# Two layers of a hybrid decoder trunk: rotary halves swapped by transfers, retention state by masked whole-array products, another order of products and steps

## The chip, the core and the metric

The kernel runs on one core of one Trainium2 chip. A core has a tensor engine (PE), a vector engine (DVE), a scalar engine (ACT), a general engine (POOL, GpSimd), and a synchronisation engine (SP) that here only issues transfers (DMAs). Each engine works through its own queue in order; semaphores hold an instruction back until what it needs from another engine or from a transfer is there. Matrix products read SBUF and write one of eight banks of PSUM; DVE and ACT read the banks. The metric is the device time of one execution in microseconds; smaller is better.

## What is computed

Two layers, each with three sub-layers on a sequence of 512 positions and a width of 1024, in float32. The mixing sub-layer has three kinds of heads:

```python
z = rmsnorm(x, mix_pre_g[i]) @ w_in[i]
# A: gated spatial mixing in chunks of 128
# B: retention, chunkwise, 6 heads of 64, with rotary positions
rq = rotary(r_q, positions); rk = rotary(r_k, positions) * 64 ** -0.5
...
def rotary(t, positions):
    ...
    t1, t2 = t[..., :half], t[..., half:]
    return jnp.concatenate([t1 * cos - t2 * sin, t1 * sin + t2 * cos], axis=-1)
def step(R, inp):      # one chunk of the retention
    q_i, k_i, v_i = inp
    inner = jnp.einsum('bhtd,bhsd->bhts', q_i, k_i) * decay
    o = jnp.einsum('bhts,bhse->bhte', inner, v_i)
    o = o + jnp.einsum('bhtd,bhde->bhte', q_i, R) * q_decay
    R = R * chunk_decay + jnp.einsum('bhsd,bhse->bhde', k_i * k_decay, v_i)
    return R, o
# C: forgetting attention, 6 heads of 64, blocks of 128 queries
x = x + rmsnorm(concat(A, B, C) @ w_o[i], mix_post_g[i])
f = conv_gated_mlp(rmsnorm(x, ffn_pre_g[i]), w_gate, w_up, conv_w, conv_b, w_down)
x = x + rmsnorm(f, ffn_post_g[i])
gate = sigmoid(rmsnorm(x, ple_pre_g[i]) @ w_ple_gate[i])
x = x + rmsnorm((p[i] @ w_ple_proj[i]) * gate, ple_post_g[i])
```

The output is x after the two layers, 512 x 1024.

## The kernel before

**A planner writes the order.** The code of `body` (L541) calls engine functions through `Plan.engine` (L138), which only records each operation with its dependencies and an estimated cost. `Plan.issue` (L252) then plays a list schedule: among the operations that are ready, an engine takes the one recorded first, and an operation that needs a new tile may be taken only if the tile's first use lies at most `AHEAD[stage]` operations (L62) behind the oldest operation not yet done, and if a buffer is free. The order that comes out is issued on L452, which is why every line of the profile says L452; operations are told apart by the names of their tiles. What is recorded earlier thus has precedence, and the engines' queues are fixed when the program is built. `fence` (L86) makes PE keep the recorded order; this holds for blocks 4 to 30 of the feed-forward part.

**Products.** Every large product splits its float32 operands in a high and a low part (`split`, L657: one ACT copy, one DVE subtraction) and takes three matmuls for one (`mm3`, L932). Pairs of projections that share their input go through `seven` (L869): seven block products in place of eight, on sums of weight blocks (`seven_weights`, L846: two 512 KB loads on SP, two adding loads on POOL's queue, sums and splits on DVE and ACT) and on sums of inputs (`Seven`, L763; `Mixed.combine`, L735). Three banks are used: beta takes b11, then h6 on top, then h7, then h4; alpha takes b21; gamma takes hd, then b22. Between the products ACT or DVE copies a bank's partial result out, and the next product on the same bank waits for that copy. In the feed-forward part some down products (`pieces`, L1322) run between b22 and h4.

**The mixing stage** (`mixers`, L965) takes its steps in the order of `STEPS` (L494): u (gating projection), F (fox values), H (sums of inputs), f0 to f2 (fox projections of head pairs), g and G (retention gates), r0 to r2 (retention projections of head pairs with the rotary turn), v (retention values), a0 to a2 (fox attention), L (silu), s (spatial gating), c0 to c2 (retention core).

- `ret_proj` (L1133): after `seven`, q and k lie as 128 partitions (two heads of 64) x 512 positions, tiles `rm`. For the rotary turn ACT writes the exchanged halves into a tile `rr`, four operations of 32 partitions for each of q and k, two of them with a minus sign (L1139, L1140); three DVE operations follow, `m*cos`, `r*sin`, and their sum.
- `ret_core` (L1146): for three chunks and two heads, a 64 x 64 state product on a part of the array (`kvps`, L1177), then a memset, a copy and two scaled sums for each head build R, whose off-diagonal blocks are zero (L1179 to L1184). R is then read by a 128x128 product for both heads.

**Output projection** (`out_proj`, L1244): chunks in the order `O_CHUNKS` (0, 2, 1, 3); the residual rows x are loaded by chunk 0, 1, 2, 3, two chunks to a buffer. After the first chunk the weights of feed-forward block 0 are asked for (`EARLY`, L496). **Feed-forward part** (`ffn`, L1274): 32 blocks of 128 columns, each one call of `seven` with some eighth part of a down product.

Of the kernel before, what the change touches and what calls it, by code (L numbers as in the profile page):

```python
# [50 lines left out]
class Plan:  # L51
# [7 lines left out]

    SETS = {"X": 17, "W": 7}  # L60

    AHEAD = {"mix": 416, "wo": 450, "wo2": 381, "emb": 503, "gu0": 443, "gu": 478, "dn": 673, "end": 164, "pg": 300, "pg2": 392}  # L62
    LOAD = 1290
    TICK = 10240 / 3
    PHASE = 1900
# [405 lines left out]
def constants():  # L471
    idx = np.arange(P, dtype=np.float64)
    lg = np.log(1.0 - 2.0 ** (-5.0 - np.arange(6, dtype=np.float64)))
    diff = idx[None, :] - idx[:, None]
    decay = np.where(diff >= 0, np.exp(lg[:, None, None] * np.maximum(diff, 0.0)), 0.0) / 8.0
    qdec = np.exp(lg[:, None] * (idx + 1.0))
    kdec = np.exp(lg[:, None] * (P - 1.0 - idx)) / 8.0
    cd = np.exp(lg * P)
    hf = np.repeat(np.arange(2), 64)
    c = {}  # L480
    c["ident"] = np.eye(P)
    c["decay"] = decay.transpose(1, 0, 2).reshape(P, 6 * P)
    c["qdec"] = np.stack([qdec[2 * p + hf] for p in range(3)], 1).reshape(P, 3 * P)
    c["kdec"] = kdec.T
    c["cd"] = np.stack([cd[2 * p + hf] for p in range(3)], 1)
    c["invf"] = (10000.0 ** (-np.arange(32, dtype=np.float64) / 32))[np.arange(P) % 32][:, None]
    c["cum"] = np.concatenate([(idx[:, None] <= idx[None, :]).astype(np.float64), np.ones((P, P))], 1)
    c["mask"] = np.where(idx[None, :] <= idx[:, None], 0.0, 1e30)
    return {k: np.ascontiguousarray(v.astype(np.float32)) for k, v in c.items()}

PAIRS = [(c + p * P, d + p * P) for c, d in ((C_RQ, C_RK), (C_FK, C_FQ)) for p in range(3)] + [(C_RG, C_RG + P)]
STEPS = "u F H f0 g f1 r0 a0 v a1 G L s r1 r2 c0 f2 c1 c2 a2"  # L494
O_CHUNKS = (0, 2, 1, 3)
EARLY = {0: 0}  # L496
O_ORDER = (5, 6, 0, 1, 2, 3, 4, 7)
IDLE = 16
SUMS_BY_DMA = True
# [41 lines left out]
def body(ctx, tc, a, out):  # L541
# [42 lines left out]


    class Rows:
        def __init__(self, src):
            self.src, self.t = src, [None, None]

        def load(self, c, queue=SY):  # L590
            if self.t[c // 2] is None:
                self.t[c // 2] = b8("x", (2, D))
            queue.dma_start(out=self[c], in_=self.src[:, c, :])

        def __getitem__(self, c):
            return self.t[c // 2][:, c % 2, :]

    x0 = a["x"][0].rearrange("(c p) d -> p c d", p=P)
    xd = [dram(f"x{i}", (P, NCH, D)) for i in range(3 * DEPTH - 1)]
# [208 lines left out]
    def post_part(src, g, out):  # L808

        n = src.shape[-1]  # L810
        s1 = small("s1", 1, bufs=12)
        A.activation(junk_t[:, 0:n], src, AF.Square, scale=D ** -0.5, accum_out=s1)
        V.tensor_tensor(out=out, in0=src, in1=g, op=ALU.mult)
        return s1
# [51 lines left out]
        split(sb[:, 0, :], sb[:, 1, :], raw[:, 1024:2048])  # L866
        return wg, wu, sa, sb

    def seven(h, ws, gs, us, scale=1.0, between=None):  # L869

        wg, wu, sa, sb = ws
        be, al, ga = (bank(n)[:, 0:256] for n in ("beta", "alpha", "gamma"))
        t1, t2 = slice(0, 256), slice(256, 512)

        def product(ps, w, n, first, last, part=range(4)):
            for k in part:
                ks = slice(k * P, k * P + P)
                mm3(ps, lambda i: w[i][:, ks], lambda i: h.part(n, i, k), first and k == 0, last and k == 3, True)

        def part(t, i):  # L880
            return [t[:, j, i * 512:i * 512 + 512] for j in range(2)]
        product(be, part(wg, 0), "b11", True, False)
        vbe, val, vga = (in_order(t) for t in (be, al, ga))
        g1, g2, u1, u2 = (halves(t[:, ts]) for t in (gs, us) for ts in (t1, t2))
        A.copy(g1, vbe)
        product(al, part(wg, 1), "b21", True, True)
        V.tensor_tensor(out=g1, in0=val, in1=g1, op=ALU.add)
        product(be, part(sa, 0), "h6", False, False)
        A.copy(g2, vbe)
        product(ga, part(sa, 1), "hd", True, False)  # L890
        if scale == 1.0:
            A.copy(u2, vga)
        else:
            A.mul(u2, vga, -scale)
        product(be, part(sb, 0), "h7", False, False)
        V.scalar_tensor_tensor(out=u2, in0=vbe, scalar=-scale, in1=u2, op0=ALU.mult, op1=ALU.subtract if scale == 1.0 else ALU.add)
        product(ga, part(sb, 1), "b22", False, True)
        V.tensor_tensor(out=g2, in0=vga, in1=g2, op=ALU.add)
# [66 lines left out]
    def mixers(l, hT, uv, ready):  # L965
# [8 lines left out]
        av = m4[:, 1024:2048].rearrange("p (c n) -> p c n", c=NCH)  # L974
        cst = m5[0:6, 0:512]
        mask = m5[:, 512:640]
        cosT = m5[:, 1536:2048]
        decay, qdec, cum, sinT = m6[:, 0:768], m6[:, 768:1152], m6[:, 1152:1408], m6[:, 1408:1920]
        for t, n in ((decay, "decay"), (qdec, "qdec"), (cum, "cum"), (mask, "mask")):
# [153 lines left out]
        def ret_proj(p):  # L1133
            res = [wk("rm") for _ in range(2)]
            seven(hT, seven_weights(a["w_fm"][l, p]), *res)
            for m in res:
                r = wk("rr")
                for s in (0, 64):
                    A.mul(r[s:s + 32, :], m[s + 32:s + 64, :], -1.0)  # L1139
                    A.copy(r[s + 32:s + 64, :], m[s:s + 32, :])  # L1140
                V.tensor_tensor(out=m, in0=m, in1=cosT, op=ALU.mult)
                V.tensor_tensor(out=r, in0=r, in1=sinT, op=ALU.mult)
                V.tensor_tensor(out=m, in0=m, in1=r, op=ALU.add)
            return res

        def ret_core(p, q, k):  # L1146
# [25 lines left out]
            kvp = bank("kvps")  # L1172
            with plan.together():
                for c in range(NCH - 1):
                    for s in range(2):
                        h = 2 * p + s
                        T.matmul(kvp[s * 64:s * 64 + 64, c * 64:c * 64 + 64], lhsT=kt[:, c * P + s * 64:c * P + s * 64 + 64], rhs=rv[:, c, h * 64:h * 64 + 64], start=True, stop=True)  # L1177
            R = wk("R", (P, 3, P))
            for s in range(2):  # L1179
                fs, off = slice(s * 64, s * 64 + 64), slice(64 - s * 64, P - s * 64)  # L1180
                G.memset(R[fs, :, off], 0.0)
                V.tensor_copy(R[fs, 0, fs], kvp[fs, 0:64])
                for c in (1, 2):
                    V.scalar_tensor_tensor(out=R[fs, c, fs], in0=R[fs, c - 1, fs], scalar=cd[fs, p:p + 1], in1=kvp[fs, c * 64:c * 64 + 64], op0=ALU.mult, op1=ALU.add)  # L1184
            ps = bank("rops")
            with plan.together():
                for c in range(NCH):
# [56 lines left out]
    def out_proj(l, cc, ready, x, new, g, nxt):  # L1244

        plan.stage = "wo"
        f = [b8("fo", (2, D)) for _ in range(2)]
        u = tm_units(a["w_wo"][l, 0], 512)
        first = [bank("wo0") for _ in range(NCH)]
        for j, k in enumerate(O_ORDER):  # L1250
            for c in range(NCH):
                tm_mm(first[c], cc, k, c, u, j == 0, j == KB - 1, j=j)
        plan.stage = "wo2"
        u = tm_units(a["w_wo"][l, 1], 512)
        plan.stage = "emb"
        emb = embed_operands(l, range(2) if l else (1,))
        plan.stage = "wo2"
        for c in range(NCH):
            x.load(c)
        first = [post_part(ps, g[:, 0, 0:512], f[c // 2][:, c % 2, 0:512]) for c, ps in enumerate(first)]  # L1260

        def done(c, ps):
            fr = f[c // 2][:, c % 2, :]
            post_chunk(x[c], (first[c], post_part(ps, g[:, 0, 512:1024], fr[:, 512:1024])), fr, stored=new[:, c, :])
            nxt(c, x[c])
            if len(seen) in EARLY:
                ready[EARLY[len(seen)]] = gate_up_weights(l, EARLY[len(seen)])
            seen.append(c)

        seen = []  # L1270
        tm_chunk_major(cc, u, 512, done, O_ORDER, O_CHUNKS)
        return emb

    def ffn(l, hs, emb, ready, x, new, g, nxt):  # L1274
# [10 lines left out]
        def gate_up(b, between):  # L1285
            ws = gate_up_weights(l, b) if b not in ready else ready[b]
            gs, us = wk("gs"), wk("us")
            seven(hs, ws, gs, us, between=between)

            cv = wk("cv")  # L1290
            A.activation(cv, gs, AF.Identity, bias=cw[:, 3, b:b + 1], scale=cw[:, 2, b:b + 1])
# [224 lines left out]
    for l in range(DEPTH):  # L1516
# [4 lines left out]
        emb = out_proj(l, cc, ready, Rows(src), xd[3 * l], g, hs)  # L1521
# [36 lines left out]
```

## Time and profile before

| | us |
|---|---|
| median of 3 runs (1526.79 to 1529.71) | 1526.82 |
| the profiled execution | 1528.62 |
| its span, first to last instruction | 1526.9 |
| start, embedding of layer 0 and first norms | 0 to 59 |
| mixing stage, layer 0 | 59 to 190 |
| output projection, layer 0 | 190 to 244 |
| feed-forward part, layer 0 | 244 to 722 |
| third sub-layer, layer 0 | 722 to 805 |
| mixing and output projection, layer 1 | 805 to 1000 |
| feed-forward part and third sub-layer, layer 1 | 1000 to 1527 |

A page of the profile gives busy times over the whole span; the stages have different limits, so the view of busy time by stage is read first, and in a stage the waits. In lines of the timeline the columns are start, duration, engine, operation, output<-inputs, shapes, count, and in brackets the idle time of the engine before it and what ended it. In the chain of waits a line is start, length and what the time was spent on. In groups of instructions the part after the first bar is busy time and mean ns, after the second the idle time before and what ended it. float32 products of small tiles appear as two records each.

### The profile page before, as it was taken

The page shows a single profiled execution, that of the slowest core. Times are in us where ns is not written, and L with a number is a line of the kernel's source. Part 1 is how long each engine was busy: PE and PEld are TensorE (multiplying, and loading weights), DVE is VectorE, ACT ScalarE, POOL GpSimd, SP SyncE. Part 2 cuts the span into 40 slices and gives each one's busy share as a digit, 9 for nine tenths or more (in the row PEclk, how much of TensorE's full clock was granted, in tenths as well). Part 3 has the DMA queues.
Part 4 walks back from the last instruction along what each step waited for, and adds up shares of the span by engine and source line. Part 5 has one row for each costly group of instructions (what it writes and reads, how often), then busy time and mean ns, then how long its engine had stood idle before and what let it go on. Part 6 is the DMA issues. An engine that isn't in the chain of part 4 may idle for free.

```text
span 1526.9 us, 26942 instructions
## 1 busy us (share of the span) xinstructions
PE 1496.3 (98%) x10554; PEld 1383.6 (91%) x10554; DVE 1216.7 (80%) x2036; ACT 888.9 (58%) x1501; POOL 194.3 (13%) x233
## 2 busy tenths in 40 slices
PE   8999999999999999999999999999999999999997
PEld 6998888899999999998889887799999999999987
DVE  6888969978778777768797779799688778778685
ACT  8557647755555545545575565587655555455462
POOL 1111102111101111100120102121101011011010
PEclk9999999999999999999999999999999999999999
DMA  9445619735646646556573355295545565465541
GB/s 335 88 135 122 209 52 280 189 90 146 173 90 175 150 117 173 146 155 245 190 197 99 92 146 182 68 334 130 146 117 153 163 149 130 123 174 139 212 174 70
DMA packets 87879, 239.02 MB, mean 157 GB/s; under 512 B 10036, under 2 KB 18364, under 8 KB 87752
## 3 DMA queue, kind: packets, MB, share of 16 engines
q1 hardware_dynamic: 64856, 195.81, 37.6%
q0 software_dynamic: 22464, 40.90, 17.0%
q8 instruction: 83, 1.36, 0.4%
q10 hardware_dynamic: 432, 0.59, 0.1%
q14 instruction: 44, 0.36, 0.1%
HBM read 219.94 MB, written 17.33 MB: 155 GB/s over the span
## 4 chain that ended last, share of the span: by engine, by line
PE 74%; DVE 8%; DMA 5%; ACT 5%; issue 5%; POOL 1%; SPq 0%; POOLq 0%; DVEq 0%; ACTq 0%
PE beta L452 20%; PE dn L452 19%; PE ps L452 13%; PE gamma L452 11%; PE alpha L452 5%; DMA graw<-in_w_gu_dram 3%; DMA traw<-in_w_dn_dram 2%; PE wo L452 1%; ACT rr L452 1%; PE hps L452 1%; DVE cv L452 1%; PE tps L452 1%; PE ops L452 1%; ACT junk L452 1%; POOL y L452 1%
## 5 line engine op out<-in xcount | busy, mean ns | idle before, releaser
L452 PE MATMUL dn<-thl,act 128*128 128x512 f32 x1536 | 351.7, 380 | 0.0
L452 PEld LDWEIGHTS dn<-thl,act 128*128 128x128 f32 x1536 | 281.8, 189 | 35.0
L452 POOL DMA_DIRECT2D graw<-in_w_gu_dram x128 | 112.1, 908 | 733.4 <-DVE wg L452 232.0
L452 PE MATMUL ps<-thl,hT 128*128 128x512 f32 (+3 forms) x984 | 198.7, 358 | 2.5 <-ACT hT L452 2.4
L452 PEld LDWEIGHTS ps<-thl,hT 128*128 128x128 f32 x984 | 171.6, 189 | 19.5 <-ACT hT L452 2.9
L452 DVE TENSOR_TENSOR thl<-traw,thl 128x1024 fp32r<-128x1024 f32 (+3 forms) x124 | 141.8, 1152 | 13.4 <-ACT thl L452 13.3
L452 ACT CAST thl<-traw 128x1024 fp32r<-128x1024 f32 (+3 forms) x124 | 121.2, 995 | 21.2 <-PE dn L452 9.2
L452 PEld LDWEIGHTS beta<-hh,wu 128*128 128x128 f32 x936 | 123.2, 191 | 7.2 <-DVE us L452 1.4
L452 PE MATMUL beta<-hh,wu 128*128 128x256 f32 x936 | 126.2, 275 | 1.0 <-DVE us L452 0.9
L452 PE MATMUL beta<-hh,wsa 128*128 128x256 f32 x936 | 120.6, 277 | 6.1 <-ACT gs L452 3.2
L452 PE MATMUL gamma<-hhd,wsa 128*128 128x256 f32 x936 | 120.8, 277 | 0.9 <-ACT wsa L452 0.8
L452 PEld LDWEIGHTS beta<-hh,wsa 128*128 128x128 f32 x936 | 111.4, 192 | 9.2 <-ACT gs L452 4.4
L452 PE MATMUL beta<-hh,wsb 128*128 128x256 f32 x936 | 118.0, 276 | 0.1
L452 DVE TENSOR_TENSOR graw<-graw 128x512 f32<-128x512 f32 x156 | 106.7, 684 | 10.4 <-DMA graw<-in_w_gu_dram 7.9
L452 PEld LDWEIGHTS gamma<-hhd,wsa 128*128 128x128 f32 x936 | 113.1, 194 | 1.3 <-ACT wsa L452 1.0
L452 PEld LDWEIGHTS beta<-hh,wsb 128*128 128x128 f32 x936 | 111.2, 193 | 0.3 <-ACT gs L452 0.3
L452 ACT CAST wsa<-graw 128x1024 fp32r<-128x1024 f32 x78 | 82.0, 1051 | 43.2 <-PE gamma L452 24.7
L452 DVE TENSOR_TENSOR wg<-graw,wg 128x1024 fp32r<-128x1024 f32 x78 | 95.1, 1219 | 13.0 <-ACT wg L452 12.8
L452 DVE TENSOR_TENSOR wsa<-graw,wsa 128x1024 fp32r<-128x1024 f32 x78 | 95.1, 1219 | 10.0 <-ACT wsa L452 9.9
L452 DVE SCALAR_TENSOR_TENSOR cv<-gs,cw,cv 128x511 f32<-128x511 f32 (+1 forms) x128 | 95.0, 743 | 8.5 <-ACT cv L452 8.2
L452 DVE TENSOR_TENSOR wsb<-graw,wsb 128x1024 fp32r<-128x1024 f32 x78 | 95.0, 1218 | 6.6 <-ACT wsb L452 5.9
L452 ACT CAST wg<-graw 128x1024 fp32r<-128x1024 f32 x78 | 82.1, 1053 | 30.5 <-PE gamma L452 13.2
(225 smaller groups left out, 2620.6 us busy)
## 6 DMA issues: line engine op xcount, KB each, us to landing
graw<-in_w_gu_dram SPq DMA_DIRECT2D x128, 512.0 KB
graw<-in_w_gu_dram POOLq DMA_DIRECT2D x128, 256.0 KB, 5.4
traw<-in_w_dn_dram SPq DMA_DIRECT2D x64, 512.0 KB
x<-x SPq DMA_DIRECT2D x40, 512.0 KB
graw<-in_w_fm_dram SPq DMA_DIRECT2D x28, 512.0 KB
traw<-in_w_wo_dram SPq DMA_DIRECT2D x16, 512.0 KB
traw<-in_w_pg_dram SPq DMA_DIRECT2D x16, 512.0 KB
graw<-in_w_fm_dram POOLq DMA_DIRECT2D x28, 256.0 KB, 5.1
```

Of the source, the lines that this page charges most:

```text
L452: made = o[1](*[self.map(v) for v in o[2]], **{k: self.map(v) for k, v in o[3].items()})
```

## The change

It has five parts.

- **Rotary halves.** The eight ACT operations of a pair's q and k become eight transfers on SP, each 32 partitions x 2 KB from SBUF to SBUF. The minus sign goes into the table of inverse frequencies, so that the sine table has it.
- **Retention state.** Three 128x128 products for both heads replace six 64x64 ones; one DVE product with a 0/1 mask `heads` (a new constant, 64 KB, loaded in each layer) takes the off-diagonal blocks away, and two scaled sums over 128 x 128 follow.
- **Seven products.** From block 4 of the feed-forward part on, hd, h6, b22, h7 replaces h6, hd, h7, b22.
- **Output projection.** x and the result tiles are paired in the order of `O_CHUNKS`, and after the fourth chunk the weights of block 1 are asked for.
- **Step order and limits.** `STEPS` and all ten `AHEAD` values.

```diff
-    AHEAD = {"mix": 416, "wo": 450, "wo2": 381, "emb": 503, "gu0": 443, "gu": 478, "dn": 673, "end": 164, "pg": 300, "pg2": 392}
+    AHEAD = {"mix": 401, "wo": 461, "wo2": 344, "emb": 430, "gu0": 423, "gu": 479, "dn": 552, "end": 208, "pg": 264, "pg2": 401}
...
-    c["invf"] = (10000.0 ** (-np.arange(32, dtype=np.float64) / 32))[np.arange(P) % 32][:, None]
+    c["invf"] = (10000.0 ** (-np.arange(32, dtype=np.float64) / 32))[np.arange(P) % 32][:, None] * np.where(np.arange(P) % 64 < 32, -1, 1)[:, None]
+    c["heads"] = hf[:, None] == hf[None, :]
...
-STEPS = "u F H f0 g f1 r0 a0 v a1 G L s r1 r2 c0 f2 c1 c2 a2"
+STEPS = "u F H f1 f0 r0 a0 v g a1 G L s r1 c0 c1 f2 r2 c2 a2"
-EARLY = {0: 0}
+EARLY = {0: 0, 3: 1}
...
     class Rows:
-        def __init__(self, src):
-            self.src, self.t = src, [None, None]
+        def __init__(self, src, order=range(NCH)):
+            self.src, self.t, self.at = src, [None, None], {c: i for i, c in enumerate(order)}
...
-        product(be, part(sa, 0), "h6", False, False)
-        A.copy(g2, vbe)
-        product(ga, part(sa, 1), "hd", True, False)
...
+        for step in (hd, h6, b22, h7) if apart else (h6, hd, h7, b22):
+            step()
...
-                for s in (0, 64):
-                    A.mul(r[s:s + 32, :], m[s + 32:s + 64, :], -1.0)
-                    A.copy(r[s + 32:s + 64, :], m[s:s + 32, :])
+                for s in range(0, P, 32):
+                    SY.dma_start(out=r[s:s + 32, :], in_=m[s ^ 32:(s ^ 32) + 32, :])
...
-                    for s in range(2):
-                        h = 2 * p + s
-                        T.matmul(kvp[s * 64:s * 64 + 64, c * 64:c * 64 + 64], lhsT=kt[:, c * P + s * 64:c * P + s * 64 + 64], rhs=rv[:, c, h * 64:h * 64 + 64], start=True, stop=True)
+                    cs = slice(c * P, c * P + P)
+                    T.matmul(kvp[:, cs], lhsT=kt[:, cs], rhs=rv[:, c, p * P:(p + 1) * P], start=True, stop=True)
             R = wk("R", (P, 3, P))
-            for s in range(2):
-                fs, off = slice(s * 64, s * 64 + 64), slice(64 - s * 64, P - s * 64)
-                G.memset(R[fs, :, off], 0.0)
-                V.tensor_copy(R[fs, 0, fs], kvp[fs, 0:64])
-                for c in (1, 2):
-                    V.scalar_tensor_tensor(out=R[fs, c, fs], in0=R[fs, c - 1, fs], scalar=cd[fs, p:p + 1], in1=kvp[fs, c * 64:c * 64 + 64], op0=ALU.mult, op1=ALU.add)
+            V.tensor_tensor(out=R, in0=kvp[:, 0:384].rearrange("p (c d) -> p c d", c=3), in1=heads.unsqueeze(1).to_broadcast([P, 3, P]), op=ALU.mult)
+            for c in (1, 2):
+                V.scalar_tensor_tensor(out=R[:, c, :], in0=R[:, c - 1, :], scalar=cd[:, p:p + 1], in1=R[:, c, :], op0=ALU.mult, op1=ALU.add)
...
+        fo = {c: f[i // 2][:, i % 2, :] for i, c in enumerate(O_CHUNKS)}
...
-        for c in range(NCH):
+        for c in O_CHUNKS:
             x.load(c)
...
-            seven(hs, ws, gs, us, between=between)
+            seven(hs, ws, gs, us, between=between, apart=b > 3)
```

More of the change, by code (lines that the diff above doesn't have):

```diff
@@ L586, in body @@
     class Rows:
-        def __init__(self, src):
-            self.src, self.t = src, [None, None]
+        def __init__(self, src, order=range(NCH)):
+            self.src, self.t, self.at = src, [None, None], {c: i for i, c in enumerate(order)}
         def load(self, c, queue=SY):
-            if self.t[c // 2] is None:
-                self.t[c // 2] = b8("x", (2, D))
+            if self.t[self.at[c] // 2] is None:
+                self.t[self.at[c] // 2] = b8("x", (2, D))
             queue.dma_start(out=self[c], in_=self.src[:, c, :])
         def __getitem__(self, c):
-            return self.t[c // 2][:, c % 2, :]
+            return self.t[self.at[c] // 2][:, self.at[c] % 2, :]
     x0 = a["x"][0].rearrange("(c p) d -> p c d", p=P)
@@ L867, in seven_weights, with seven @@
         return wg, wu, sa, sb
-    def seven(h, ws, gs, us, scale=1.0, between=None):
+    def seven(h, ws, gs, us, scale=1.0, between=None, apart=False):
         wg, wu, sa, sb = ws
@@ L887, in seven, with h6, hd, h7 @@
         V.tensor_tensor(out=g1, in0=val, in1=g1, op=ALU.add)
-        product(be, part(sa, 0), "h6", False, False)
-        A.copy(g2, vbe)
-        product(ga, part(sa, 1), "hd", True, False)
[L891 to L898, printed above, removed]
+        def h6():
+            product(be, part(sa, 0), "h6", False, False)
+            A.copy(g2, vbe)
+        def hd():
+            product(ga, part(sa, 1), "hd", True, False)
+            if scale == 1.0:
+                A.copy(u2, vga)
+            else:
+                A.mul(u2, vga, -scale)
+        def h7():
+            product(be, part(sb, 0), "h7", False, False)
+            V.scalar_tensor_tensor(out=u2, in0=vbe, scalar=-scale, in1=u2, op0=ALU.mult, op1=ALU.subtract if scale == 1.0 else ALU.add)
+        def b22():
+            product(ga, part(sb, 1), "b22", False, True)
+            V.tensor_tensor(out=g2, in0=vga, in1=g2, op=ALU.add)
+        for step in (hd, h6, b22, h7) if apart else (h6, hd, h7, b22):
+            step()
         rest = between() if between else None
@@ L976, in mixers @@
         mask = m5[:, 512:640]
+        heads = m5[:, 640:768]
         cosT = m5[:, 1536:2048]
         decay, qdec, cum, sinT = m6[:, 0:768], m6[:, 768:1152], m6[:, 1152:1408], m6[:, 1408:1920]
-        for t, n in ((decay, "decay"), (qdec, "qdec"), (cum, "cum"), (mask, "mask")):
+        for t, n in ((decay, "decay"), (qdec, "qdec"), (cum, "cum"), (mask, "mask"), (heads, "heads")):
             SY.dma_start(out=t, in_=a["c_" + n])
@@ L1257, in out_proj @@
         plan.stage = "wo2"
-        for c in range(NCH):
+        for c in O_CHUNKS:
             x.load(c)
-        first = [post_part(ps, g[:, 0, 0:512], f[c // 2][:, c % 2, 0:512]) for c, ps in enumerate(first)]
+        first = [post_part(ps, g[:, 0, 0:512], fo[c][:, 0:512]) for c, ps in enumerate(first)]
         def done(c, ps):
-            fr = f[c // 2][:, c % 2, :]
+            fr = fo[c]
             post_chunk(x[c], (first[c], post_part(ps, g[:, 0, 512:1024], fr[:, 512:1024])), fr, stored=new[:, c, :])
@@ L1520, in body @@
         hs = Seven(g)
-        emb = out_proj(l, cc, ready, Rows(src), xd[3 * l], g, hs)
+        emb = out_proj(l, cc, ready, Rows(src, O_CHUNKS), xd[3 * l], g, hs)
         g = Gains(("ffn_post_g", l), ("ple_pre_g", l))
```

## The prediction

> **What bounds the kernel now.** I read the page's busy times first, then the busy times by stage, then the waits of the tensor engine, and last the order of time around each wait.
>
> ```profile
> PE 1496.3 (98%) x10554; PEld 1383.6 (91%) x10554; DVE 1216.7 (80%) x2036; ACT 888.9 (58%) x1501; POOL 194.3 (13%) x233
> ```
>
> The tensor engine (PE) is busy for 1496.3 of 1526.9 us. Whatever happens elsewhere is worth at most the 30.6 us in which PE stands still, plus any slow PE work. So the question is where those 30.6 us lie. The view of busy time by stage tells it; its columns are the stretch, its length, the busy time of PE, weight load, DVE, ACT and POOL, the granted clock, the DMA share and GB/s:
>
> ```profile
> core 0: us, PE busy (x) PEld busy (x) DVE busy (x) ACT busy (x) POOL busy (x), PEclk, DMA share, GB/s
> 0.00:59.00 59.00, 53.89 (x272) 44.28 (x273) 43.15 (x68) 41.72 (x74) 8.36 (x17) 1.00 0.83 267
> 98.00:141.00 43.00, 41.49 (x271) 34.36 (x270) 35.89 (x129) 30.51 (x66) 5.52 (x8) 1.00 0.40 98
> 298.00:691.00 393.00, 391.58 (x2912) 374.26 (x2912) 304.63 (x422) 213.00 (x327) 41.94 (x48) 1.00 0.55 143
> 845.00:889.00 44.00, 42.65 (x285) 35.37 (x285) 34.49 (x126) 30.80 (x67) 4.05 (x6) 1.00 0.32 75
> 889.00:968.00 79.00, 75.11 (x552) 63.32 (x550) 66.48 (x152) 45.38 (x83) 11.15 (x11) 1.00 0.48 148
> 1049.00:1445.00 396.00, 393.84 (x2914) 375.16 (x2914) 306.33 (x423) 213.68 (x328) 42.93 (x50) 1.00 0.55 144
> 1476.00:1527.00 51.00, 43.03 (x231) 38.24 (x229) 33.74 (x58) 21.56 (x41) 6.18 (x8) 0.97 0.24 86
> ```
>
> The start (5.1 us idle) and the end (8.0 us idle) are not touched by the change. That leaves 30.6 - 13.1 = 17.5 us. The two long feed-forward stretches, 789 us together, stand still for only 1.4 and 2.2 us. The mixing stages lose 1.5, 1.4 and 3.9 us. Most of the rest lies where the feed-forward part begins (below). No single bottleneck is to be removed here; there are some forty small stalls, and the change touches the cause of several.
>
> **Part A: the seven products in another order (from block 4 on).** Now the product h6 follows b21 directly and adds into the bank that ACT has to copy after b11. ACT has the time of one product for that. Which waits end late is shown by the groups of instructions, shapes kept apart:
>
> ```profile
> L452 PE MATMUL beta<-hh,wsa 128*128 128x256 f32 x936 | 120.6, 277 | 6.1 <-ACT gs L452 3.2 <-DVE wsa L452 2.6 <-ACT fqk L452 0.2
> ```
>
> 3.2 us of PE waits stand before h6, released by ACT's copy to gs. The longest, in the chain of waits (start, length, what) and in the order of ACT's work:
>
> ```profile
> 400.30 8.29 DMA traw<-in_w_dn_dram
> ...
> 409.56 0.61 ACT act L452
> 410.18 0.28 ACT gs L452
> ...
> 410.50 1.60 PE beta L452 x12
> ...
> 297.76 4.75 PE dn L452 x22
> ...
> 395.87 1.34 PE gamma L452 x12
> ...
> 410.35 1.05 ACT L452 CAST wsa<-graw 128x1024 fp32r<-128x1024 f32 x1
> ```
>
> A late load of down weights (8.29 us) holds up ACT's queue, the copy stands behind it, PE waits. In the new order hd runs between, on another bank: 12 more matmuls, 1.34 us of cover as the running gamma group shows. Five such waits hold 3.2 us, and the first group after a wait takes 1.60 where a running one takes 1.50 (its row stands under B): at most 3.2 + 5 x 0.1 = 3.7 us. But the next thing that PE needs is then ACT's copy of hd's bank, and casts of 1.05 us each stand in ACT's queue behind the gs copy; the longest wait may come back one product later. I take **-2.9**, bounds -3.7 and -1. What the new order puts at risk is the DVE step after h7, which h4 waits for: the down matmuls lie between (22 in 4.75 us), so it is hidden at all blocks but the last, where PE is free to take down matmuls first. If that cover were gone, it would cost up to the 1.34 us of one product, the cover that the step has now, in each of 28 blocks of a layer.
>
> **Part B: block 1's weights asked for in the output projection.** The start of the feed-forward part:
>
> ```profile
> 200.00:230.00 30.00, 29.41 (x151) 24.34 (x150) 18.40 (x29) 13.16 (x28) 2.55 (x4) 1.00 0.11 27
> 240.00:290.00 50.00, 47.18 (x393) 45.19 (x391) 48.45 (x74) 39.17 (x66) 11.65 (x13) 1.00 0.89 257
> 1010.00:1040.00 30.00, 29.11 (x260) 28.92 (x260) 29.99 (x46) 25.83 (x41) 5.30 (x6) 1.00 0.92 269
> ...
> 290.73 1.53 PE L452 MATMUL beta<-hh,wsa 128*128 128x256 f32 x10 [2.25 <-DVE wsa L452]
> 292.06 2.77 PE L452 MATMUL gamma<-hhd,wsa 128*128 128x256 f32 x12
> 294.63 1.80 PE L452 MATMUL beta<-hh,wsb 128*128 128x256 f32 x12
> 296.26 1.50 PE L452 MATMUL gamma<-hb,wsb 128*128 128x256 f32 x12
> ...
> L452 DVE TENSOR_TENSOR wg<-graw,wg 128x1024 fp32r<-128x1024 f32 x78 | 95.1, 1219 | 13.0 <-ACT wg L452 12.8
> L452 DVE TENSOR_TENSOR graw<-graw 128x512 f32<-128x512 f32 x156 | 106.7, 684 | 10.4 <-DMA graw<-in_w_gu_dram 7.9
> ```
>
> From 240 to 290 DVE is busy 48.45 of 50 us and the DMA engines 0.89; PE loses 2.8 us there and the end of the 2.25 us wait after it, some 3.5 in all. Just before, from 200 to 230, DVE has 11.6 us free and DMA stands at 0.11. One block's weights are three DVE steps of 1.22 us and three of 0.68 (two sums and the split of wu, which has graw's width), 5.7 us: they fit into that hole if buffers come free for them. The 2.25 us wait has a tail: the next groups take 1.53 for 10 matmuls (1.28 at the running pace), 2.77 for 12 and 1.80 (1.50 each), in all 1.8 us of slow clock. The second layer loses 0.9 in 1010 to 1040. So at most 3.5 + 1.8 + 0.9 = 6.2 us can go. The limits for what may be allocated ahead are cut as well (gu0 443 to 423), which works against it by 20 instructions, but the request moves up by far more: the embedding product and the whole of block 0 were ahead of it. I take **-4.0**, bounds -6.2 and 0.
>
> [...]
>
> **Part C: the rotary halves by transfers.** ACT's four small operations for each tensor, and what waited for them:
>
> ```profile
> L452 ACT ACTIVATE rr<-rm x24: 627/630/634, 97.6 to 916.2; 32x512 f32<-32x512 f32 x24
> L452 ACT COPY rr<-rm x24: 615/618/627, 98.2 to 916.9; 32x512 f32<-32x512 f32 x24
> ...
> 105.26 0.69 DVE L452 TENSOR_TENSOR rm<-rm,mix 128x512 f32<-128x512 f32 x1 [1.58 <-ACT rr L452]
> ...
> 106.81 0.33 PE L452 MATMUL tps<-k_ident,pe 128*128 128x128 f32 x1 [1.51 <-DVE fet L452]
> ...
> 853.86 0.33 PE L452 MATMUL tps<-k_ident,pe 128*128 128x128 f32 x1 [1.35 <-DVE fet L452]
> ...
> 902.66 0.49 PE L452 MATMUL gamma<-hhd,wsa 128*128 128x256 f32 x2 [0.84 <-ACT wsa L452]
> ...
> 904.22 1.16 PE L452 MATMUL ips<-rm 64*128 64x128 f32 x16 [0.79 <-DVE rm L452]
> ```
>
> 24 x 0.630 + 24 x 0.618 = 30 us leave ACT. DVE waits for them in its queue, the copy for attention (fet) stands behind, and PE waits: 1.51 + 1.35 + 0.84 + 0.79 = 4.5 us of PE time come from there. In their place come 48 transfers of 64 KB from SP, four a tensor. The nearest rows:
>
> ```profile
> 73.44 1.77 SPq L452 DMA_DIRECT2D cums<-mix  x6
> 75.32 0.82 SPq L452 DMA_DIRECT2D fcb<-cums  x2
> ```
>
> Six issues take 1.77 us (0.295 each), and the first of them had landed when its reader was issued 1.88 us after it. So one tensor is swapped in 4 x 0.295 + 1.9 = 3.1 us in a quiet moment, where ACT takes 2.5; the pair in 4.3, where ACT takes 5.0. At the other end stands the 8.29 us of the load above, with work ahead of it in the queues. DVE's product with the cosine overwrites the source, so it waits for all four, and behind it in DVE's queue stand the softmax steps of fox attention. Weight loads queued behind the copies on SP lose 0.3 us each copy, 14 us in all, on an engine that mostly waits. I take the row of the quiet moment, since DMA is at 0.40 and 0.48 in these stages: some of the 4.5 us goes, some comes back as a wait for a landing. **-2.5**, bounds -4.5 and +6 (the price of late copies, below).
>
> **Part D: the state by whole-array products.**
>
> ```profile
> 159.31 0.57 PE L452 MATMUL kvps<-mix,kt 128*64 128x64 f32 x12
> 159.81 0.38 PE L452 MATMUL beta<-hT,wg 128*128 128x256 f32 x1
> ...
> 162.20 0.44 PE L452 MATMUL rops<-R,qd 128*128 128x128 f32 x2
> 162.48 0.56 PE L452 MATMUL rops<-mix,inn 128*128 128x64 f32 x4
> ```
>
> Now the six half-array products (12 records) take 0.50 us to the next start, and some 0.2 for going into that form and out of it. One 128x128 product takes 162.48 - 162.20 = 0.28; three take 0.84. So PE loses 0.14 to 0.34 for each of six pairs. **+0.9**, bounds +0.8 and +2.0. On DVE six small operations become three and two memsets leave POOL; DVE is not at its limit in these stages (35.89 of 43, 66.48 of 79), so nothing is gained on the path. The added mask constant is 64 KB in each layer, issued beside constants that are there already: 0.
>
> **Part E: step order, limits, chunk order.** The stalls of the second mixing stage not explained above are 3.9 - 1.6 = 2.3 us; a new order moves such stalls about and can make as many. c2 now follows r2 at once, but a2 and the output projection stand ready to fill. **0**, bounds -3 and +4. The folded sign of the sine adds no instruction: 0.
>
> **Sum.** -2.9 - 4.0 - 2.5 + 0.9 + 0 = -8.5 us. The profiled execution took 1528.6 us with a span of 1526.9, some 1.7 lying around it; the median of the runs shown is 1526.8. I subtract from the median: **1518.3 us**.
>
> **Rivals.** First, *the stalls only change place* (1523.8 to 1529.8). Block 1's weights find no free buffers before 230 us, so B stays near 0, and the landing of the copies takes the place of ACT in C. Left are A and D: 1526.8 - 2.9 + 0.9 = 1524.8. For it: DVE is full at the start of both feed-forward parts whatever is asked for. Against it: the hole of 30 us with DMA at 0.11. Chance 0.18.
>
> Second, *slower: the copies queue behind weights*.
>
> ```profile
> 900.40 8.23 SPq L452 DMA_DIRECT2D traw<-in_w_wo_dram  x6
> ```
>
> Just where the last rotary steps run, SP issues six 512 KB loads for the output projection. At the 269 GB/s seen above, 3.1 MB are 11.7 us of transfer; copies issued behind them land some 8.3 us later instead of 2.5, about 6 us late, with 1.8 us of slow clock behind a PE stall of that length: 7.8 us. If that falls on r1 or r2 twice in the two layers, it is 15.6 us and C's gain is gone: 1526.8 - 8.5 + 2.5 + 15.6 = 1536.4. It decides from two such hits on; one leaves it faster or the same. Against it: the kernel's planner counts bytes in one line, and PE has output-projection products to fill with. Chance 0.12.
>
> Third, *nearly all goes* (below 1512): A, B and C at their far ends and half of E, -3.7 - 6.2 - 4.5 + 0.8 - 1.5 = -15.1, 1511.7. Chance 0.06.
>
> The forecast, 1512 to 1523.7, has the remaining 0.64. So faster by over 0.2% (0.2%, 3.1 us, is about what a measurement of this kernel can tell from no change) has 0.70, within 0.2% has 0.18, slower has 0.12. The range goes from 1511 to 1529: it leaves out most of the slower case and the last of the third.
>
> **What would show it.** A: h6's group loses its 3.2 us behind ACT gs, and no wait behind DVE us appears before h4. B: in layer 0 the splits of a second block's wg lie before 240 us, and the 2.25 us wait and the slow clock after it are gone. C: the waits of tps on fet shrink, and no DVE operation on rr waits long for a DMA; a wait of over 3 us there means the second rival. D: 36 records of 128x128 in place of 72 small ones, pace 0.14 us. The prediction is wrong if PE's idle time between 60 and 1476 us is still above 14 us.

## The result, and the profile after

The changed kernel takes 1512.8 us (median of 4 runs, 1511.13 to 1517.87) where the kernel before took 1528.26 beside it: ratio 0.9902, 95% interval 0.9876 to 0.9929, some 15 us faster. That lies in the range (1511 to 1529) and on the side that was forecast, but nearly twice as far from the start as the 8.5 us of the sum. The profiled execution has a span of 1509.8 us, 17.1 less than before; it took 1511.49 us, 1.3 less than its median, where that of before took 1528.62, so the two profiles differ by more than the medians do.

The busy times of the page, after:

```profile
PE 1487.8 (99%) x10518; PEld 1383.0 (92%) x10518; DVE 1208.9 (80%) x2018; ACT 861.5 (57%) x1453; POOL 193.8 (13%) x221
```

PE stands still for 1509.8 - 1487.8 = 22.0 us, 8.6 less than before. It is also busy for 8.5 us less, though its products are the same but for the state. So the idle time fell by as much as the whole sum of the prediction (8.5 us), though not where its terms had put it, as the section on the prediction shows. The other half of the gain is busy time, which the sum priced only in part: 0.1 us for each wait in A and 1.8 us of slow clock in B.

By stage, after (length, then busy PE, weight load, DVE, ACT, POOL, granted clock, DMA share, GB/s):

```profile
core 0: us, PE busy (x) PEld busy (x) DVE busy (x) ACT busy (x) POOL busy (x), PEclk, DMA share, GB/s
...
95.00:138.00 43.00, 42.59 (x313) 37.74 (x313) 37.03 (x113) 26.16 (x54) 8.13 (x7) 1.00 0.45 109
...
237.00:291.00 54.00, 51.63 (x436) 49.84 (x435) 51.95 (x79) 42.41 (x71) 10.00 (x11) 1.00 0.83 246
291.00:684.00 393.00, 391.50 (x2909) 374.19 (x2908) 306.63 (x426) 215.51 (x329) 44.68 (x51) 1.00 0.54 141
...
836.00:880.00 44.00, 44.00 (x323) 38.24 (x322) 36.52 (x113) 28.31 (x59) 8.03 (x6) 1.00 0.41 104
880.00:950.00 70.00, 69.29 (x518) 61.92 (x517) 62.65 (x140) 34.29 (x62) 9.17 (x6) 1.00 0.60 186
...
1030.00:1428.00 398.00, 395.26 (x2938) 377.58 (x2938) 310.29 (x430) 217.69 (x334) 45.53 (x52) 1.00 0.55 144
```

The mixing stages now idle for 0.4, 0.0 and 0.7 us where they idled for 1.5, 1.4 and 3.9. The long feed-forward stretches idle for 1.5 and 2.7: no less than before. The waits of PE, after (us in total, times, longest):

```profile
PE beta L452 <- ACT gs L452: 4.1, 3, 1.5
PE hps L452 <- DVE h L452: 3.4, 5, 1.2
PE ps L452 <- ACT hT L452: 2.4, 2, 1.5
...
PE tps L452 <- DVE pe L452: 0.4, 1, 0.4
```

The waits of tps for fet (2.9 us) and of h6 for wsa (2.6 us) are gone; those for ACT's copy to gs have not shrunk, three now hold 4.1 us. Where the time went, by the start of landmark products in the timelines (us), for the two kernels and, for later, six of the experiments:

| | before | after | n_plus | a_rot | a_state | u_ahead | b_plus | u_rot |
|---|---|---|---|---|---|---|---|---|
| last product of output projection, layer 0 | 237.4 | 233.2 | 235.8 | 238.8 | 235.9 | 241.8 | 242.8 | 239.9 |
| first down product, layer 0 | 297.6 | 290.5 | 298.3 | 296.7 | 295.7 | 302.3 | 303.4 | 300.4 |
| last down product, layer 0 | 721.4 | 714.2 | 722.5 | 720.1 | 720.5 | 728.3 | 730.7 | 727.5 |
| last product of output projection, layer 1 | 988.9 | 973.5 | 984.5 | 981.8 | 986.1 | 989.9 | 999.6 | 988.6 |
| first down product, layer 1 | 1048.8 | 1033.3 | 1044.1 | 1040.6 | 1044.8 | 1051.7 | 1059.3 | 1050.4 |
| last down product, layer 1 | 1475.3 | 1458.7 | 1467.7 | 1465.8 | 1468.5 | 1474.5 | 1484.2 | 1474.0 |
| end | 1526.9 | 1509.8 | 1518.7 | 1517.0 | 1519.5 | 1525.5 | 1535.7 | 1525.0 |

By the unrounded starts of the first two columns, 4.2 us are gained up to the end of layer 0's output projection, 3.0 at the start of its feed-forward part, 0.2 in the rest of it, 8.1 in the third sub-layer, mixing and output projection after that, 0.1 and 1.0 in the second feed-forward part, 0.6 at the end. Each column is one execution: that of u_rot took 2.6 us more than the median of its runs, and that of b_plus 3.8 us more.

### The profile page after: what moved, and what is told of

Same layout as the page of the kernel before. It is cut to its first block, busy times and chain, and to the rows that moved or that the text cites. A ratio compares the mean times of both kernels' runs of the same rounds, so it can differ in the third digit from the quotient of the medians.

```text
span 1509.8 us, 26837 instructions
## 1 busy us (share of the span) xinstructions
PE 1487.8 (99%) x10518; PEld 1383.0 (92%) x10518; DVE 1208.9 (80%) x2018; ACT 861.5 (57%) x1453; POOL 193.8 (13%) x221
## 3 DMA queue, kind: packets, MB, share of 16 engines
q8 instruction: 82, 1.34, 0.4%
## 4 chain that ended last, share of the span: by engine, by line
PE 85%; DMA 6%; DVE 4%; issue 2%; ACT 2%; SPq 1%; POOL 1%; POOLq 0%; DVEq 0%; ACTq 0%
PE beta L452 24%; PE dn L452 21%; PE ps L452 12%; PE gamma L452 12%; PE alpha L452 6%; DMA graw<-in_w_gu_dram 3%; PE wo L452 2%; PE hps L452 1%; PE eps L452 1%; PE sps L452 1%; PE ops L452 1%; PE tps L452 1%; PE rops L452 1%; PE gps L452 1%; SPq L452 1%
## 5 line engine op out<-in xcount | busy, mean ns | idle before, releaser
L452 DVE TENSOR_TENSOR facc<-dn,facc 128x512 f32<-128x512 f32 x112 | 76.8, 687 | 53.5 <-PE dn L452 53.1
L452 PE MATMUL beta<-hb,wg 128*128 128x256 f32 x768 | 98.0, 276 | 0.1
L452 PE MATMUL alpha<-hb,wg 128*128 128x256 f32 x768 | 96.9, 275 | 0.5 <-ACT hb L452 0.5
L452 PE MATMUL gamma<-hb,wsb 128*128 128x256 f32 x768 | 96.5, 275 | 0.5 <-ACT us L452 0.4
```

The source lines that it names most:

```text
L452: made = o[1](*[self.map(v) for v in o[2]], **{k: self.map(v) for k, v in o[3].items()})
```

## The experiments

Theory 1 was that the parts of the change carry the gain, above all the transfers in the mixing stages. Theory 2 was that the order which the planner makes carries much of it. Ratios are to the kernel before, run beside each on the same chip; the changed kernel's is 0.9902.

| run | what it is | median us | ratio | 95% interval |
|---|---|---|---|---|
| u_rot | changed, ACT swaps the halves | 1524.15 | 0.9962 | 0.9948 to 0.9976 |
| u_state | changed, half-array state | 1522.35 | 0.9953 | 0.9936 to 0.9970 |
| u_seven | changed, old order of products | 1514.47 | 0.9899 | 0.9883 to 0.9915 |
| u_wo | changed, no early block 1, old chunk pairs | 1517.32 | 0.9917 | 0.9896 to 0.9937 |
| u_ahead | changed, old limits | 1527.89 | 1.0000 | 0.9990 to 1.0010 |
| n_plus | changed, mix limit 405 | 1522.27 | 0.9959 | 0.9944 to 0.9974 |
| n_minus | changed, mix limit 393 | 1511.45 | 0.9893 | 0.9875 to 0.9911 |
| n_seven | n_minus, old order of products | 1521.19 | 0.9948 | 0.9935 to 0.9961 |
| a_rot | before, transfers swap the halves | 1519.45 | 0.9937 | 0.9924 to 0.9951 |
| a_state | before, whole-array state | 1521.21 | 0.9952 | 0.9938 to 0.9966 |
| b_plus | before, mix limit 420 | 1533.54 | 1.0032 | 1.0020 to 1.0044 |
| b_minus | before, mix limit 408 | 1526.93 | 0.9987 | 0.9977 to 0.9997 |

**Undoing one part of four.** u_rot:

```diff
-                for s in range(0, P, 32):
-                    SY.dma_start(out=r[s:s + 32, :], in_=m[s ^ 32:(s ^ 32) + 32, :])
+                for s in (0, 64):
+                    A.mul(r[s:s + 32, :], m[s + 32:s + 64, :], -1.0)
+                    A.copy(r[s + 32:s + 64, :], m[s:s + 32, :])
```

> The changed kernel with the rotary halves swapped by ACT again, all else as changed. Theory 1 (the transfers took the stalls out of the mixing stages, which became 11.9 us shorter in all): most of that is lost, the ratio to the kernel before rises from 0.990 to 0.995 or more (1520 us), and PE again waits behind ACT rr or DVE fet in both mixing stages. Rival (the step order and the limits did it, whoever swaps the halves): the loss is below 3 us, ratio below 0.992.

u_state puts the six 64x64 products, the copies, sums and memsets of before back (the reverse of the state part of the diff above).

> The changed kernel with the six half-array state products, the copies and memsets of before. By the prediction's part D the whole-array products cost PE 0.8 to 2.0 us, so this should be 1 us faster (ratio 0.9895). Rival: leaving the half-array form costs PE more than its own time, and the shorter chain to R matters, so this is 1 to 4 us slower (ratio 0.991 to 0.993).

u_seven:

```diff
-            seven(hs, ws, gs, us, between=between, apart=b > 3)
+            seven(hs, ws, gs, us, between=between)
```

> The changed kernel with the products in the order of before in all blocks. By the prediction's part A it loses 2.9 us (ratio 0.992) and PE waits for ACT gs before h6 come back. Rival, from the trace of the changed kernel, where three waits for ACT gs hold 4.1 us in other places: the order only moves the wait by a product, and the loss is below 1 us.

u_wo:

```diff
-EARLY = {0: 0, 3: 1}
+EARLY = {0: 0}
...
-        for c in O_CHUNKS:
+        for c in range(NCH):
             x.load(c)
```

> The changed kernel without the early request for block 1 and with x and the results paired by chunk number as before. By the prediction's part B it loses 3 to 5 us (ratio 0.992 to 0.9935), and in layer 0 a wait of over 2 us for DVE wsa with slow clock behind it returns before the first down product. Rival (the limits gu0, emb and wo2 alone gave the 3.0 us that the stretch became shorter): below 1 us.

By their times u_rot and u_state lose 9.2 and 7.8 us (0.0060 and 0.0051 of 1528), u_wo 2.3, u_seven nothing. Read alone, that would make the rotary and the state part worth the whole gain. But what was to be seen in the traces came only in part. In u_rot, where ACT swaps the halves again, PE does not wait for fet at all; it waits 1.0 us for a rotary turn (DVE rm). u_state loses more than either of its two expectations. In u_seven no wait for ACT gs before h6 comes back; PE waits 3.5 us for ACT us instead, most of it before b22. u_wo lies between its two expectations, and its long wait is for DVE us (3.4), that for DVE wsa being 1.1. Then the control.

**The control: one limit, nothing else.**

```diff
-    AHEAD = {"mix": 401, ...
+    AHEAD = {"mix": 405, ...
```

> Control: the changed kernel with nothing but the limit of the mixing stage raised from 401 to 405, so that no operation is added, removed or made dearer, and only the plan's order moves. If the parts themselves carry the gain (theory 1), this stays within 2 us of the changed kernel (ratio 0.989 to 0.9915). If the plan's order carries much of it (theory 2: any upset of the order loses several us, and the losses of 8 to 9 us on undoing one part tell little of the part), it loses 4 us or more (ratio 0.993 and up).

> The same control to the other side, 401 to 393. Theory 1: ratio 0.989 to 0.9915. Theory 2: it lies elsewhere again, 0.992 to 0.998, with other stalls in other places.

n_plus loses 8.7 us (0.0057), as much as taking out a part; that is what theory 2 said. n_minus gives 0.9893, where theory 1 put it, and not the 0.992 to 0.998 of theory 2: not every shift of the limit upsets the order. Two stalls of n_plus are also found in u_rot. The waits of PE in u_rot and, below, in n_plus:

```profile
PE beta L452 <- ACT wg L452: 2.4, 2, 2.1
...
PE beta L452 <- DVE wsa L452: 2.1, 1, 2.1
...
PE ips L452 <- DVE rm L452: 1.0, 1, 1.0
```

```profile
PE beta L452 <- ACT wg L452: 2.1, 1, 2.1
...
PE beta L452 <- DVE wsa L452: 2.0, 1, 2.0
...
PE ips L452 <- DVE rm L452: 0.9, 1, 0.9
```

The first two are the same stalls, at the start of layer 0's feed-forward part: 2.12 us between the same two products, and 2.09 and 2.02 us before the same product of the second block. The third is not: it lies in layer 0 in u_rot (157.22 us) and in layer 1 in n_plus (934.90 us). Timelines of u_rot and of n_plus:

```profile
251.97 0.49 PE L452 MATMUL beta<-hb,wg 128*128 128x256 f32 x2 [2.12 <-ACT wg L452]
...
268.94 0.60 PE L452 MATMUL beta<-hh,wsa 128*128 128x256 f32 x3 [2.09 <-DVE wsa L452]
```

```profile
247.92 0.49 PE L452 MATMUL beta<-hb,wg 128*128 128x256 f32 x2 [2.12 <-ACT wg L452]
...
265.37 0.98 PE L452 MATMUL beta<-hh,wsa 128*128 128x256 f32 x3 [2.02 <-DVE wsa L452]
```

n_plus swaps its halves by transfers, so these stalls do not need ACT's four operations: 4.2 us of idle time in u_rot can come from an upset plan alone. Theory 1 fails in its simple form: a loss upon undoing a part is not that part's worth here.

**The limits, and the state part alone.** u_ahead replaces the line of all ten limits by that of before; a_state is the kernel before with the state part of the diff.

> The changed kernel with all ten limits of before. Theory 1: the limits are worth little, the ratio stays below 0.993. Theory 2: most of the gain goes with them, ratio 0.995 or more. Part B says besides that the larger gu0 limit should not hurt the start of the feed-forward part.

> The kernel before with only the whole-array state products, their mask and the sums over 128 x 128. Prediction, part D: +0.8 to +2.0 us (ratio 1.0005 to 1.0013). The loss of 8 us on undoing it, read as the part's worth, would give 0.995. Theory 2: somewhere within 4 us of the kernel before, by the order that comes out.

With the old limits all of the gain is gone, as theory 2 said. The early request for block 1 is still there, and yet layer 0's feed-forward part takes 60.5 us to its first down product, as long as before (60.2; changed 57.3): what part B said of the larger limit did not hold. What such a limit decides is seen at r2 in layer 0. In u_ahead PE waits 5.32 us for the end of the rotary turn of r2 (timeline of u_ahead):

```profile
175.58 4.96 SPq L452 DMA_DIRECT2D rr<-rm  x8
...
179.74 0.27 PE L452 MATMUL tps<-k_ident,pe 128*128 128x128 f32 x1
185.34 2.08 PE L452 MATMUL ips<-rm 64*128 64x128 f32 x16 [5.32 <-DVE rm L452]
```

In the changed kernel the same product comes at the same time, and PE works up to it (its timeline):

```profile
174.73 5.93 SPq L452 DMA_DIRECT2D rr<-rm  x8
...
179.16 6.07 PE L452 MATMUL wo<-thl,cc 128*128 128x512 f32 x27
185.16 1.16 PE L452 MATMUL ips<-rm 64*128 64x128 f32 x16
```

The chain is not shorter: 185.16 against 185.34. The difference at this place, 5.3 of the 15 us, is 27 products of the output projection that the plan had put there. That the copies waited behind weights is not it either: DMA stood still just before them (u_ahead by stage):

```profile
170.00:175.00 5.00, 5.00 (x47) 5.00 (x46) 4.50 (x7) 1.65 (x3) 0.74 (x1) 1.00 0.00 0
175.00:180.00 5.00, 5.00 (x36) 3.14 (x34) 3.84 (x17) 3.54 (x9) 0.89 (x1) 1.00 0.28 69
180.00:186.00 6.00, 0.68 (x7) 0.69 (x8) 6.00 (x17) 1.03 (x5) 0.00 (x0) 0.93 0.77 250
186.00:190.00 4.00, 4.00 (x27) 3.31 (x26) 3.32 (x13) 0.97 (x3) 0.00 (x0) 0.67 1.03 385
```

a_state is 7.3 us faster than before (0.0048), where part D said 0.9 slower and theory 2 at most 4 us either way; the loss on undoing the part, read as its worth, would give 0.995, and that is what came. The waits for fet and for rr's successors are still there (2.8, 0.8), as nothing touched them. The landmarks show its 7.4 us of span spread over the run: 1.4 up to the end of layer 0's output projection, 1.9 in the third sub-layer, mixing and output projection after layer 0's feed-forward part, 1.1 at the start of the second feed-forward part, 2.7 in the rest of that. The last two lie where no retention runs.

**The spread of the kernel before, the rotary part alone, and part A again.** b_plus and b_minus change only the mix limit of the kernel before, from 416 to 420 and 408; a_rot is the kernel before with the transfers and the folded sign; n_seven is n_minus with the edit of u_seven.

> The kernel before with nothing but the limit of the mixing stage raised from 416 to 420. If the spread that one limit makes is a property of the planner and not of the change, this moves by several us too (ratio below 0.997 or above 1.003). If the kernel before is insensitive, it stays within 0.998 to 1.002.

> The same to the other side, 416 to 408. If the parts of the change carry a gain of their own, all orders of the old parts stay above those of the new ones: no ratio below 0.995 here, while the new parts gave 0.989 to 0.996 for three limits. If the order alone does it, a ratio of 0.99 to 0.995 can turn up here.

> The kernel before with only the rotary halves by transfers. Prediction, part C: -2.5 us (ratio 0.998), from -4.5 to +6. The waits of PE behind DVE fet at the first attention step (2.9 us before) should shrink if ACT's four operations caused them. The loss of 9 us on undoing the part, read as its worth, would give 0.994. Rival 2 of the prediction would show as a wait of over 3 us behind the copies.

> The changed kernel with the mixing limit 393 (0.9893 above) and the products in the order of before: part A a second time, under another order of the rest. Part A of the prediction gives a loss of 2.9 us (ratio 0.991). That the order only moves the wait gives 0.988 to 0.990, and if it is the fastest of all, it is the version to keep.

The limit moves the kernel before, too: 1.0032, 1, 0.9987 for 420, 416, 408. With all new parts the same play gives 0.9959, 0.9902, 0.9893. The two sets do not overlap, and their means differ by 0.0088, 13 us. So the new parts with their limits do better for more than one order; three orders each are few, and u_ahead shows a set of limits with which the new parts give nothing. Of the two expectations, b_plus, just beyond the 1.003 that was named, and b_minus bear out both: the spread is the planner's, and no order of the old parts came below 0.995.

a_rot gains 9.6 us (0.0063) against the 2.5 of part C. Its waits for fet are gone and no wait behind a copy is longer than 1.0 us (waits of PE in a_rot, and tile rr):

```profile
PE gamma L452 <- ACT us L452: 3.8, 3, 2.1
PE hps L452 <- DVE h L452: 3.7, 8, 0.6
...
PE tps L452 <- DVE nm L452: 0.3, 1, 0.3
```

```profile
L452 SPq DMA_DIRECT2D rr<-rm x48: 507/588/956, 97.9 to 910.6; - x48
...
  ACT rm L452: 1.0, 1
  ACT wu L452: 0.6, 1
  DVE rm L452: 0.6, 1
```

But by the landmarks it is 1.4 us later than before at the end of layer 0's output projection, then makes up 2.3 at the start of the feed-forward part and 5.7 between the two feed-forward parts: the effect of the part and that of the order are mixed here as well.

Added alone, the two parts give 9.6 and 7.3 us; undone, they cost 9.2 and 7.8. The sums agree, which speaks for theory 1, but the places do not. u_rot loses 6.7 us up to the end of layer 0's output projection, where a_rot gains nothing, and only 1.7 us between the feed-forward parts, where a_rot gains 5.7.

That stretch, from layer 0's last down product to the end of layer 1's output projection, is where the change as a whole gains most, 8.1 us, and there the gain stands up under every order at hand. It takes 266.8 to 268.8 us in the three kernels with all the old parts, 265.6 in a_state, 261.8 in a_rot, and 259.4 to 262.1 in all nine kernels with the new step order, u_rot (261.1), u_state (261.2), u_wo (260.1) and u_ahead (261.6) among them. So none of the parts undone here is needed for it where the step order is new, and the transfers alone get most of it under the old one. No run has the new step order alone; what it is worth by itself is open.

n_seven loses 8.4 us to n_minus where u_seven lost nothing to the changed kernel. Its largest new stall lies at the start of the second feed-forward part (timeline of n_seven):

```profile
1021.91 0.49 PE L452 MATMUL gamma<-hhd,wsa 128*128 128x256 f32 x2 [0.84 <-ACT wsa L452]
...
1024.69 1.68 PE L452 MATMUL beta<-hh,wsa 128*128 128x256 f32 x9 [2.02 <-DVE wsa L452]
```

That is among the first four blocks, where the order of the products is the same in both, and the start of that feed-forward part takes 4.6 us longer than in n_minus: more than half of the loss is order, not the part. In the two long stretches after the starts, where the part acts, n_seven takes 1.0 and 1.2 us longer than n_minus; u_seven, against the changed kernel, 0.2 less and 0.8 more.

## Why the prediction was right, and where its sum was not

**Bound: right. Place: half right.** PE's idle time was the thing to win. Idle time between 60 and 1476 us fell from 17.5 to under 10, below the 14 that was named as the point of failure. But A and B had 6.9 of the 8.5 us in the feed-forward parts, which became 4.3 us shorter, starts included; the stages before them became 12.3 us shorter, where C, D and E together had 1.6.

**The price of a stall: too low in every term.** Terms A, B and C counted the idle time; A added 0.1 us for each wait, and only B the slow clock. The changed kernel has 8.6 us less idle time and 8.5 us less busy time. Two things in its trace would explain most of the second, by an estimate. One stall, in the changed kernel's timeline:

```profile
1392.79 1.50 PE L452 MATMUL beta<-hh,wsa 128*128 128x256 f32 x12
1394.13 1.50 PE L452 MATMUL gamma<-hb,wsb 128*128 128x256 f32 x12
1397.02 1.60 PE L452 MATMUL beta<-hh,wsb 128*128 128x256 f32 x12 [1.38 <-ACT gs L452]
```

A running group of 12 is shown as 1.50 us and hands over after 1.34, its end lying beside the next group's start; before a stall the last 0.16 stand alone, and the group after takes 0.10 more. So a stall of 1.38 costs 1.64. The timeline of before has 42 idle gaps of PE above 40 ns, that of after 22: 20 x 0.26 = 5.2 us, if each costs what this one does. The one stretch of slow clock inside the run, 0.66 from 291 to 296 us of before, is gone, 1.8 us. Together 7.0 of the 8.5; the state products add 0.85; what else is in the rest was not separated.

**Part A (-2.9): not borne out.** "hd runs between" was so, and h6's wait fell from 3.2 to 1.3 us, but a wait came back. The same paragraph had feared it one product later, for the copy of hd's bank (ACT us), where there are now 0.4 us; it stands two products later, in front of h7, for the copy behind h6 (groups of PE instructions, shapes apart, after):

```profile
L452 PE MATMUL beta<-hh,wsa 128*128 128x256 f32 x936 | 120.6, 276 | 1.3 <-ACT gs L452 1.3
L452 PE MATMUL beta<-hh,wsb 128*128 128x256 f32 x936 | 118.3, 276 | 2.9 <-ACT gs L452 2.9
L452 PE MATMUL beta<-hh,wu 128*128 128x256 f32 x936 | 126.4, 275 | 0.3 <-DVE us L452 0.3
```

1.3 + 2.9 in place of 3.2. u_seven, without the part, takes the same time. In the stretches where it acts, the part spares 0.6 us against u_seven and 2.2 under the order of n_minus, less than the 2.9. With either order of products PE stalls at about the same blocks, for one copy of ACT or another: three waits hold 4.6 us in n_seven, 3.3 in n_minus and 4.1 in the changed kernel. The cover of the DVE step before h4 held: 0.3 us.

**Part B (-4.0): the number came near, the cause is likely but not shown.** The two starts became 3.0 and 0.1 us shorter, 3.1 in all. The loads of block 1 moved from 231 to 195 us, and the wait of 2.25 us with its slow clock is gone. But the hole was hardly used: the split of block 1's wg starts at 239.2 us, just inside the 240 that was named as the sign, and at 240.1 in u_wo, which asks for block 1 late. The start of layer 0's feed-forward part takes 56.6 to 57.3 us in five kernels with the part, but 60.5 in u_rot and u_ahead and 62.4 in n_plus, which have it too. It takes 59.8 to 61.1 us in five kernels without the part, but 57.9 in a_rot. That leans towards the part, and the order of the plan can still undo its effect or have the same effect without it. Without the early request and the new pairing, u_wo has a wait of 3.42 there and a slower group behind it (its timeline):

```profile
283.68 1.88 PE L452 MATMUL beta<-hh,wu 128*128 128x256 f32 x12 [3.42 <-DVE us L452]
```

Its loss, 2.3 us, has an interval that overlaps with that of the changed kernel, so the time does not settle it either.

**Part C (-2.5): the mechanism shown in a_rot alone, its size was not right.** The waits of 2.9 us on fet are gone in a_rot, which differs from the kernel before by the transfers and the folded sign only. For the changed kernel that proves little, since they are gone in u_rot as well, where ACT swaps the halves under the new step order. In the changed kernel DVE waits 1.3 us in all for copies. One number was off: an issue takes 0.588 us at the median (0.507 to 1.577 in the changed kernel), not 0.295, which was read off transfers of a single row of 2 KB; eight take 5 to 6 us. In the changed kernel POOL once waited 7.0 us for this tile, PE never. Alone the part gave 9.6 us. The second rival, copies behind weights, was not seen in the traces; the one long wait behind a rotary turn (5.32 us) had another cause.

**Part D (+0.9): near for the products, partly by luck, and wrong for the whole.** The products cost PE 0.85 us more in all six pairs together, by the distance from each product's start to the next (2.99 us in sum before, 3.84 after), 0.14 a pair. But the six records of a pair now take 0.59 to 0.67 us and not 0.84, and the price of going into the half-array form, which the prediction had taken off, lies outside this count. It can be seen at the products just in front, in the timelines of before and, below, after:

```profile
173.16 0.39 PE L452 MATMUL gamma<-hT,wsb 128*128 128x256 f32 x2
173.47 0.57 PE L452 MATMUL kvps<-mix,kt 128*64 128x64 f32 x12
```

```profile
146.79 0.39 PE L452 MATMUL beta<-hT,wg 128*128 128x256 f32 x2
147.02 0.83 PE L452 MATMUL kvps<-mix,kt 128*128 128x128 f32 x6
```

Two products take 0.31 us to the first state product before and 0.23 after, so some 0.08 of the 0.14 comes back. But the part also takes eight operations from each pair out of a plan whose limits count operations. With the order that came of it, a_state is 7.3 us faster, not 0.9 slower.

**Part E (0, bounds -3 to +4): the failed step.** "a new order moves such stalls about and can make as many" gave it far too little weight: the term was put at 0, within -3 and +4. Four steps of one limit cost 8.7 us and all ten old limits 15 us, more than any other term of the sum.

That the time fell into the range thus owes something to luck: the sum says nothing of which order comes out, A and D were not borne out as said, and with the same parts the time is 1522.3 us with the mixing limit at 405 and 1527.9 with the old limits.

What stays open is how the 15 us divide. The parts do not add up: undone one at a time they cost 9.2, 7.8, -0.5, 2.3 and 15.0 us, 34 in all. Each edit changes the plan, and with the same operations the orders at hand differ by up to 11 us when only the mixing limit is moved, and by 16 when all ten limits are. The step order, the first half of part E, was never changed alone, though the stretch that gains most goes with it. To tell a part's own worth one would have to hold the order fixed, which these runs did not do.

## What to carry to other kernels

Where a planner or a search makes the order, run a control that changes the order and nothing else before reading anything from an ablation: here it moved the time as much as the parts did, and it showed by two equal stalls that part of a loss was not the part's. Compare not only how much is lost and gained but where. Price a PE stall above its idle time: in this kernel by an estimated quarter of a microsecond, and by an estimated 1.7 us more where the clock dropped. A long chain need not be shortened if products from another stage can be put beside it: 27 of them hid 6 us.

## What the runs showed of the hardware

Behind some stalls of PE the granted clock dropped, in four drops for 3.4 to 3.5 us, and the length of one wait alone did not bring it down: a stall of 2.12 us came with a drop in n_plus and without one in u_rot. The kernel before shows a whole drop, behind its stall of 2.25 us, which ends at 290.73:

```profile
284.00:291.00 7.00, 4.75 (x40) 4.53 (x41) 7.00 (x10) 5.60 (x10) 1.78 (x2) 1.00 0.29 67
291.00:296.00 5.00, 5.00 (x32) 5.00 (x32) 4.69 (x7) 3.70 (x7) 0.87 (x2) 0.66 0.99 252
296.00:298.00 2.00, 2.00 (x18) 1.97 (x18) 1.46 (x2) 0.72 (x1) 0.89 (x1) 1.00 1.05 408
```

Stretches of b_plus around three of its stalls, of 2.25, 1.95, and 1.24 with 0.46 soon after, then one of a_rot around a stall of 2.14:

```profile
296.00:300.00 4.00, 3.44 (x21) 3.44 (x22) 4.00 (x6) 3.39 (x6) 0.00 (x0) 0.73 1.00 261
607.00:611.00 4.00, 3.50 (x20) 3.51 (x21) 3.55 (x5) 1.77 (x4) 0.86 (x1) 0.68 0.33 64
863.00:868.00 5.00, 3.88 (x14) 3.68 (x15) 4.36 (x23) 3.12 (x9) 0.00 (x0) 0.66 0.01 2
```

```profile
1388.00:1396.00 8.00, 5.86 (x42) 5.41 (x41) 4.58 (x7) 4.32 (x6) 0.88 (x1) 1.00 0.64 145
```

The 2.14 us stall in a_rot brought no drop. The plainest comparison is the stall of 2.12 us that n_plus and u_rot share, between the same two products; two stretches of n_plus, the first inside the drop and the second over the stall, then one of u_rot over the stall and what follows it:

```profile
249.00:251.00 2.00, 2.00 (x10) 2.00 (x11) 1.54 (x4) 0.33 (x1) 1.43 (x2) 0.50 0.96 352
247.00:252.00 5.00, 3.97 (x19) 3.68 (x20) 3.77 (x5) 2.33 (x3) 2.61 (x3) 0.66 1.02 376
```

```profile
247.00:256.00 9.00, 6.38 (x50) 5.80 (x51) 6.89 (x11) 4.75 (x9) 3.16 (x4) 1.00 0.92 307
```

Equal stalls, one with a drop and one without. Inside the drop of n_plus the clock stands at 0.50, so 5 us at a mean of 0.66, in before, in n_plus and in the last stretch of b_plus, are 3.4 us of slow clock; u_ahead's two stretches after its 5.32 us wait (0.93 over 6, 0.67 over 4) give 0.8 + 2.6 = 3.5. So these four drops lasted 3.4 to 3.5 us whether the stalls were 1.7 (1.24 and 0.46) or 5.3 us, and by this estimate cost half of that in work. The 4 us stretches of b_plus, at 0.73 and 0.68, hold 2.2 and 2.6 us of slow clock; what lies outside them is not shown. One drop lasted twice as long (0.51 over 7 us), in u_state after stalls of 1.86 and 0.56 us:

```profile
211.00:218.00 7.00, 6.28 (x22) 4.35 (x20) 6.93 (x22) 2.78 (x8) 1.19 (x2) 0.51 0.48 79
```
